# The per-layer gate and the router written as three products of high and low parts

## The chip, the cores and the metric

The kernel runs on one core of a Trainium2 chip. The metric is the device time of one execution in microseconds (us), the median of several runs. The engines are TensorE (PE: matmuls; its weight loads stand apart as PEld), VectorE (DVE), ScalarE (ACT), GpSimd (POOL) and SyncE (SP), which here only issues transfers from main memory.

## The reference, cut to what matters

The program is a two-layer block (feed-forward, mixers, attention) followed by one block with a mixture of experts, on 256 positions (two halves of 128, called t = 0 and 1) with 1024 features, all in 32-bit floats. The change lies in the last part of the second block:

```python
h = layer_norm_2(DEEPNORM_ALPHA_2 * h + y, ln1_g[i], ln1_b[i])
e = jnp.matmul(p[i], ple_proj[i]) * jax.nn.sigmoid(jnp.matmul(h, ple_gate[i]))
m = moe_ffn(h, w_router, router_bias, exp_w_up[i], exp_w_down[i])
h = layer_norm_2(DEEPNORM_ALPHA_2 * h + m + e, ln2_g[i], ln2_b[i])
...
aff = jax.nn.sigmoid(jnp.matmul(xt, w_router).astype(jnp.float32))      # in moe_ffn
```

`ple_gate` (1024 x 1024) is the gate of the per-layer input; `w_router` (1024 x 16) chooses two of 16 experts for each position. An expert has an up matrix of 1024 x 1024 and a down matrix of 512 x 1024.

## The kernel before, in words

**Two kinds of product.** Most products before the mixture are written as three products of parts: each operand is split into a high part, rounded to the type fp32r by ACT (`split`, L593), and a low part, the rest, by DVE (L594), and PE adds high x high, high x low and low x high (`mm3`, L598 to L600). For weights of the stream (`ws`) the casts are L298 and the subtractions L306. In the last part, the gate, the router and the experts are plain 32-bit float products.

**The weights of the last part** come in tiles of 128 x 2048 floats (1 MB), 102 of them, numbered in the order of their use: 0 and 1 are the left half of the gate, 2 the left half of the projection (`wp`, half as large), 3 to 8 expert 0 (four of up, two of down), 9 to 14 expert 1, 15 and 16 the right half of the gate, 17 the right half of the projection, 18 to 23 expert 2, and so on up to 96 to 101 of expert 15. `wtile` gives a tile its place in memory. The first `MOE_TILES` = 17 tiles have places of their own: 4 early ones (`w0` to `w3`), 4 slots of the stream's ring (a slot is a pair of half tiles, `wh` and `wl`), 3 buffers `raw` of the stream, and 6 more ring slots. A ring slot comes free when its last piece of the stream has been used, a `raw` buffer when its pieces have been split. From tile 17 on a tile takes the place of one that was given back with `moe_free`, in that order; SP issues all these loads in the order of the program (L245), and each waits until its place is free.

**The order of the work around the change** (`second`, L1790 and on) is that of the program on every engine. PE runs the out projection `w2`: for half 0, then for half 1. While it runs for half 1, DVE normalises half 0 (`ln_math`, L675 to L685, gain and bias in `gb`, loaded by SP). PE then turns the normalised X0 (`xT_plain`, into `xh`), runs `router(0)` (L1787) and five eighths of the gate's left half for t = 0 (`gate`, L1937). DVE meanwhile normalises X1. PE turns X1, ends the gate for t = 0, runs `router(1)` and the gate for t = 1. In `routing` DVE ranks the experts in some thirty short steps (from L1981 to L2009), PE counts positions (L2012 to L2016), DVE builds the selection S (L2091), and PE gathers the positions of the first four experts (`gather_quad`, L2104).

**The loop over 16 experts** (`moe`) follows: up products (L2135), then the down products (L2158) of the expert before, and the combining. After expert 0 stands the left projection, ahead of expert 2 (`GATE_AT`) the gate's right half for both t and the right projection.

Of the kernel before, what the change touches and what calls it, by code (L numbers as in the profile page):

```python
# [17 lines left out]
KT = 8  # L18
# [143 lines left out]
ALPHA2 = 2.0 ** 0.25  # L162
MOE_TILES = 17
MOE_EARLY = 4
# [345 lines left out]
class Kernel:  # L510
# [1245 lines left out]
    def w2(self, ks, ts, mid=None):  # L1756
        for k in ks:
            h, w = self.st.get(("w2", k))
            for t in ts:
                s = slice(t * P, (t + 1) * P)  # L1760
                for i in range(2):
                    c = slice(i * 512, (i + 1) * 512)
                    self.mm3(self.wacc[t][i], self.mix[0][:, k, s], self.mix[1][:, k, s], h[:, c], w[:, c],
                             k == 0, k == 7)
            if ts[-1]:
                self.st.release(("w2", k))
                self.moe_adv()
            self.st.pump(1)
            if mid and k == mid[0]:
                mid[1]()  # L1770

    def xT_plain(self, t, ss=(0, 1)):
        nc = self.nc
        for s in ss:
# [4 lines left out]
            pv = pt.rearrange("p (k n) -> p k n", k=4)  # L1779
            nc.scalar.copy(self.xf[:, 4 * s:4 * s + 2, t * P:(t + 1) * P], pv[:, 0:2])  # L1780
            nc.vector.tensor_copy(self.xf[:, 4 * s + 2:4 * s + 4, t * P:(t + 1) * P], pv[:, 2:4])

    def router(self, t):
        if t == 0:
            self.rps = self.mm()
        for k in range(KT):
            self.nc.tensor.matmul(self.rps[:, 16 * t:16 * t + 16], self.xf[:, k, t * P:(t + 1) * P],  # L1787
                                  self.rw[:, 16 * k:16 * k + 16], start=k == 0, stop=k == KT - 1)

    def second(self, g, acc, fs, fe):  # L1790
# [37 lines left out]
        self.ln_math(0, self.wacc[0], s2, e2)  # L1828
        self.xf = self.common.tile([P, KT, T], F32, name="xh")
        self.w2(range(2, 8), (1,), (6, lambda: self.xT_plain(0, (0,))))  # L1830
        self.xT_plain(0, (1,))
        self.p_T()
        self.m2ctx.close()
        self.moe_load(MOE_TILES)
        self.pe = self.pool("expert", 1, self.moectx, side="right")
# [21 lines left out]
    def moe_open(self):  # L1857
# [18 lines left out]
        self.wkind = [("early", f"w{i}", 0) for i in range(MOE_EARLY)]  # L1876
        self.wkind += [("ring", i % RING, i) for i in range(at - RING + RING_LESS, at)]
        self.wkind += [("raw", "raw", 0)] * RAWB
        self.wkind += [("ring", self.st.slot(i)[0], i) for i in range(n - RING_LESS, n)]
        assert len(self.wkind) == MOE_TILES  # L1880
        self.moe_load(MOE_EARLY)

    def wtile(self):
        i = len(self.wslot)
        s = i if i < MOE_TILES else self.wslot[self.wfree[i - MOE_TILES]]
        self.wslot.append(s)
# [26 lines left out]
    def moe_adv(self):  # L1913
        st = self.st
        while len(self.wtiles) < MOE_TILES:
# [3 lines left out]
            self.moe_load(len(self.wtiles) + 1)  # L1919

    def moe_free(self, tiles):
        self.wfree += tiles
        self.moe_load(MOE_TILES + len(self.wfree))

# [8 lines left out]
    def gate(self, i, t, ks):  # L1933
        for k in ks:
            w = self.wtiles[GATE_TILES[2 * i + k // 4]]
            c = k % 4 * 512
            self.nc.tensor.matmul(self.gacc[t], self.xf[:, k, t * P:(t + 1) * P], w[:, c:c + 512],  # L1937
                                  start=k == 0, stop=k == 7)

# [243 lines left out]
    def moe(self):  # L2183
        nc = self.nc
        self.nmm = 3
        self.gate_out()
        self.moe_free(GATE_TILES[:2])
        xg = self.gather_quad(0)
# [5 lines left out]
        for e in range(16):  # L2194
            if e == GATE_AT:
# [6 lines left out]
                next(ple)  # L2202
                self.moe_free(GATE_TILES[2:] + PROJ_TILES[1:])
            ps = self.mm()
# [36 lines left out]
            if e % 2 == 0:  # L2241
                self.prep(e // 2)
            if e in (7, 8):
                next(spill)
# [227 lines left out]
```

## Time and profile before

| what | value |
|---|---|
| time, median of 3 runs (lowest, highest) | 1537.07 us (1536.45 to 1538.68) |
| profiled execution, its own time | 1537.33 us |
| span of its profile, first to last instruction | 1535.5 us |
| PE busy | 1503.7 us, 98% of the span |
| DVE, ACT busy | 885.0 us, 654.2 us |
| read from main memory | 330.34 MB |

The span is what the trace shows; the 1.8 us between it and the execution's own time lie outside the program. All stretches are counted in us from the first instruction. The stretch of the change begins with half 1 of `w2` at about 1243 us and ends with the last expert at about 1522 us. PE's ends are modelled, so that a PE without idle time is best read from the starts of its instructions.

### The profile page before, as it was taken

How to read it: one execution, taken by the hardware profiler on the slowest of the kernel's cores; microseconds unless marked ns; L12 is line 12 of the kernel's file. 1: busy time of each engine (PE TensorE's matmuls, PEld its weight loads, DVE VectorE, ACT ScalarE, POOL GpSimd, SP SyncE). 2: the span in 40 equal slices, each digit the busy share in tenths (PEclk: the TensorE clock that was granted, in tenths of full speed). 3: DMA queues.
4: the chain of work that ended last, by engine and by line, in shares of the span. 5: the costliest groups of instructions: out<-in, count | busy, mean ns of one | idle time of the engine just before them, and what ended most of it. 6: DMA issues, size and time to landing. Idle time of an engine off the chain costs nothing. (4 is left out here: it accounts for less than half of the span.)

```text
span 1535.5 us, 23692 instructions
## 1 busy us (share of the span) xinstructions
PE 1503.7 (98%) x9717; PEld 1241.3 (81%) x9718; DVE 885.0 (58%) x1410; ACT 654.2 (43%) x1060; POOL 39.4 (3%) x61
## 2 busy tenths in 40 slices
PE   9999999999999999999999999999999999999996
PEld 7999989889999899998878999967989974434432
DVE  5644567785455745458857555568888465222223
ACT  5544435454443534336653434465774431111111
POOL 0000000000000000001001000020000000000000
PEclk9999999999999999999999999999999999999999
DMA  8654535555545554536334654545544677899991
GB/s 305 231 222 180 192 111 219 192 195 191 190 175 182 211 197 172 206 138 230 125 127 188 219 186 172 192 135 179 211 147 177 232 274 294 338 416 418 416 416 72
DMA packets 56130, 332.98 MB, mean 217 GB/s; under 512 B 6337, under 2 KB 6657, under 8 KB 24657
## 3 DMA queue, kind: packets, MB, share of 16 engines
q1 hardware_dynamic: 53568, 319.68, 55.4%
q0 software_dynamic: 1872, 9.52, 1.7%
q10 hardware_dynamic: 576, 2.22, 0.4%
q8 instruction: 78, 1.28, 0.3%
q14 instruction: 36, 0.29, 0.1%
HBM read 330.34 MB, written 1.05 MB: 216 GB/s over the span
## 5 line engine op out<-in xcount | busy, mean ns | idle before, releaser
L306 DVE TENSOR_TENSOR wl<-raw,wh 128x1024 fp32r<-128x1024 f32 (+1 forms) x403 | 474.1, 1216 | 130.4 <-ACT wh L298 130.0
L298 ACT CAST wh<-raw 128x1024 fp32r<-128x1024 f32 (+1 forms) x404 | 403.6, 1044 | 136.8 <-PE acc L600 45.6
L608 PE MATMUL mm<-xh,wh 128*128 128x256 f32 x1608 | 454.4, 283 | 2.0 <-DVE big L962 1.1
L609 PE MATMUL mm<-xl,wh 128*128 128x256 f32 x1608 | 451.7, 281 | 0.0
L610 PE MATMUL mm<-xh,wl 128*128 128x256 f32 x1608 | 451.2, 281 | 0.0
L608 PEld LDWEIGHTS mm<-xh,wh 128*128 128x128 f32 x1608 | 303.4, 189 | 7.5 <-issue 1.8
L609 PEld LDWEIGHTS mm<-xl,wh 128*128 128x128 f32 x1608 | 303.0, 188 | 2.0
L610 PEld LDWEIGHTS mm<-xh,wl 128*128 128x128 f32 x1608 | 303.5, 189 | 0.0
L422 ACT ACTIVATE fs<-mm 128x256 f32<-128x256 f32 x80 | 30.8, 385 | 280.6 <-PE mm L610 280.6
L424 DVE TENSOR_TENSOR fm<-fs,mm 128x256 f32<-128x256 f32 x80 | 33.6, 421 | 198.7 <-ACT fs L422 198.7
L599 PE MATMUL acc<-wl,fhh 128*128 128x512 f32 x352 | 139.1, 395 | 0.0
L598 PE MATMUL acc<-wh,fhh 128*128 128x512 f32 x352 | 138.9, 395 | 0.0
L600 PE MATMUL acc<-wh,fhl 128*128 128x512 f32 x352 | 138.5, 394 | 0.0
L600 PEld LDWEIGHTS acc<-wh,fhl 128*128 128x128 f32 x352 | 66.1, 188 | 15.6
L598 PEld LDWEIGHTS acc<-wh,fhh 128*128 128x128 f32 x352 | 66.3, 188 | 13.2
L599 PEld LDWEIGHTS acc<-wl,fhh 128*128 128x128 f32 x352 | 66.1, 188 | 12.8
L594 DVE TENSOR_TENSOR fhl<-fm,fhh 128x256 fp32r<-128x256 f32 x80 | 34.0, 426 | 37.7 <-ACT fhh L593 37.7
L2139 ACT ACTIVATE es<-mm 128x256 f32<-128x256 f32 x16 | 6.1, 384 | 109.1 <-PE mm L2135 109.1
L593 ACT CAST fhh<-fm 128x256 fp32r<-128x256 f32 x80 | 32.5, 406 | 45.1 <-DVE fm L424 45.1
L2173 DVE SCALAR_TENSOR_TENSOR X<-mm,ws,X 64x512 fp32r<-64x512 f32 x32 | 24.0, 750 | 42.5 <-ACT X L2170 41.9
L661 POOL TENSOR_TENSOR rs_r<-rs_v,nhalf 128x1 f32<-128x1 f32 (+3 forms) x21 | 17.8, 848 | 1167.0 <-DVE rs_v L659 1127.8
L2170 ACT ACTIVATE X<-mm,ws 64x512 fp32r<-64x512 f32 x32 | 21.9, 683 | 53.9 <-PE mm L2158 53.6
(603 smaller groups left out, 2112.5 us busy)
## 6 DMA issues: line engine op xcount, KB each, us to landing
raw<-in_ws_dram SPq DMA_DIRECT2D x196, 1024.0 KB, 4.9
wh<-in_we_dram SPq DMA_DIRECT2D x57, 512.0 KB, 11.3
wl<-in_we_dram SPq DMA_DIRECT2D x57, 512.0 KB, 11.2
w<-in_we_dram SPq DMA_DIRECT2D x22, 1024.0 KB, 11.9
raw<-in_we_dram SPq DMA_DIRECT2D x17, 1024.0 KB, 11.3
gb<-in_lnp_dram POOLq DMA_DIRECT2D x5, 1024.0 KB, 5.0
w<-in_wg_dram SPq DMA_DIRECT2D x2, 1024.0 KB, 7.5
raw<-in_ws_dram SPq DMA_DIRECT2D x2, 896.0 KB, 4.6
```

The source lines that it names most:

```text
L298: self.nc.scalar.copy(h[:, :n], src)
L306: self.eng.tensor_sub(l, src, h)
L422: nc.scalar.activation(s[:, :n], ps[:, :n], AF.Silu)
L424: nc.vector.tensor_tensor(m[:, :n], s[:, :n], ps[:, n:2 * n], op=OP.mult)
L593: self.nc.scalar.copy(h, src)
L594: self.nc.vector.tensor_sub(l, src, h)
L598: mm(out, lh, rh, start=first, stop=False)
L599: mm(out, lh, rl, start=False, stop=False)
L600: mm(out, ll, rh, start=False, stop=last)
L608: mm(out, h[:, c], xh[:, k, s], start=k == 0, stop=False)
L609: mm(out, h[:, c], xl[:, k, s], start=False, stop=False)
L610: mm(out, l[:, c], xh[:, k, s], start=False, stop=k == kn - 1)
```

## The change

The gate's and the router's products become `mm3`, three fp32r products each. For that:

- X0 and X1, when turned, are split into `xf` (high, ACT) and `xl2` (low, DVE); `xl2` takes the third `raw` buffer.
- The router's weights `rw` are split once, in `router(0)`.
- The gate's weight tiles are split in halves of 128 x 1024 by a generator, `presplit`, into four ring slots (`wh` and `wl` of each: the high and the low part). Tiles 0 and 1 are split in four steps during `w2` for half 1, tile 15 at the end of expert 0, tile 16 at the end of expert 1. A tile's place is given back as soon as it is split.
- These four ring slots and the third `raw` buffer are no longer among the first places, so that `MOE_TILES` is 12; they join (as -1 to -5 in `moe_free`) after the gate's right half.

```diff
-MOE_TILES = 17
+MOE_TILES = 12
...
             self.st.pump(1)
+            if not ts[0] == 0 and 1 < k < 6:
+                next(self.gsplit)
...
-            nc.scalar.copy(self.xf[:, 4 * s:4 * s + 2, t * P:(t + 1) * P], pv[:, 0:2])
-            nc.vector.tensor_copy(self.xf[:, 4 * s + 2:4 * s + 4, t * P:(t + 1) * P], pv[:, 2:4])
+            for k in (0, 2):
+                d = slice(None), slice(4 * s + k, 4 * s + k + 2), slice(t * P, (t + 1) * P)
+                self.split(self.xf[d], self.xl2[d], pv[:, k:k + 2])
...
+        if t == 0:
+            self.rhl = self.pe.tile([P, 2, P], F32R, name="eh", bufs=2)
+            self.split(self.rhl[:, 0], self.rhl[:, 1], self.rw)
         for k in range(KT):
-            self.nc.tensor.matmul(self.rps[:, 16 * t:16 * t + 16], self.xf[:, k, t * P:(t + 1) * P],
-                                  self.rw[:, 16 * k:16 * k + 16], start=k == 0, stop=k == KT - 1)
+            s, c = slice(t * P, (t + 1) * P), slice(16 * k, 16 * k + 16)
+            self.mm3(self.rps[:, 16 * t:16 * t + 16], self.xf[:, k, s], self.xl2[:, k, s], self.rhl[:, 0, c],
+                     self.rhl[:, 1, c], k == 0, k == KT - 1)
...
+    def presplit(self, i):
+        for t in GATE_TILES[2 * i:2 * i + 2]:
+            for h in range(2):
+                j = self.nstage % 4
+                hi, lo = [self.ringp.tile([P, 1024], F32R, name=s) for s in self.stages[2 * j:2 * j + 2]]
+                self.split(hi, lo, self.wtiles[t][:, h * 1024:(h + 1) * 1024])
+                self.wsplit[t, h] = hi, lo
+                self.nstage += 1
+                if h:
+                    self.moe_free([t])
+                yield
...
         for k in ks:
-            w = self.wtiles[GATE_TILES[2 * i + k // 4]]
-            c = k % 4 * 512
-            self.nc.tensor.matmul(self.gacc[t], self.xf[:, k, t * P:(t + 1) * P], w[:, c:c + 512],
-                                  start=k == 0, stop=k == 7)
+            h, l = self.wsplit[GATE_TILES[2 * i + k // 4], k % 4 // 2]
+            c, s = slice(k % 2 * 512, k % 2 * 512 + 512), slice(t * P, (t + 1) * P)
+            self.mm3(self.gacc[t], self.xf[:, k, s], self.xl2[:, k, s], h[:, c], l[:, c], k == 0, k == 7)
...
-        self.moe_free(GATE_TILES[:2])
+        next(self.gsplit, None)
+        self.gsplit = self.presplit(1)
...
-                self.moe_free(GATE_TILES[2:] + PROJ_TILES[1:])
+                self.moe_free([-1, -2, -3, -4, -5] + list(PROJ_TILES[1:]))
...
+            if e < GATE_AT:
+                next(self.gsplit)
+                next(self.gsplit)
```

DVE between the end of X0's normalisation (L685 on `X_72`) and the start of X1's (L675 on `X_73`), removed rows with -, new ones with +; `wl` from `w` is a low part of the gate's tiles 0 and 1, `raw` is `xl2`, `eh` the router's low part:

```order
 L685 SCALAR_TENSOR_TENSOR X_72<-X_72,rs_r,gb 128x512
-L1781 COPY xh<-acc 128x2x128 x2
-L1837 CAST identr<-ident 128x128
+L594 TENSOR_TENSOR wl_12616<-w_11646,wh_12615 128x1024
+L594 TENSOR_TENSOR wl_12630<-w_11646,wh_12629 128x1024
+L594 TENSOR_TENSOR wl_12644<-w_11648,wh_12643 128x1024
+L594 TENSOR_TENSOR wl_12658<-w_11648,wh_12657 128x1024
+L594 TENSOR_TENSOR raw<-acc,xh 128x2x128 x4
+L1848 CAST identr<-ident 128x128
+L594 TENSOR_TENSOR eh<-rw,eh 128x128
 L675 SCALAR_TENSOR_TENSOR X_73<-acc,X_73 128x512 x2
```

Nine subtractions now stand between the two normalisations, where two copies stood; the router's low part is the last of them.

SP around the load of `gb` for these normalisations; `in_ws` is the stream, `in_we` the experts' weights, and the removed ring rows shown are the last two of eight:

```order
-L245 DMA wh_12384<-in_we_dram 128x1024
-L245 DMA wl_12385<-in_we_dram 128x1024
-L285 DMA raw<-in_ws_dram 128x2048
-L245 DMA raw<-in_we_dram 128x2048 x3
+L285 DMA raw<-in_ws_dram 128x2048 x9
+L245 DMA raw<-in_we_dram 128x2048 x2
 L586 DMA gb<-in_lnp_dram 128x2048
```

Four ring tiles ahead of the last block of the stream are gone, and one load of 1 MB less stands ahead of `gb`.

SP from tile 13 to tile 20 in the changed kernel, with what each waits for (DMAHW: an earlier transfer; PE, DVE: the last use of the place):

```order
L245 DMA w_12710<-in_we_dram 128x2048 [waits DMAHW6_49,DVE_49]
L245 DMA w_13035<-in_we_dram 128x2048 [waits DMAHW7_49,PE_49]
L245 DMA raw<-in_wg_dram 128x2048 [waits DMAHW0_49,PE_49]
L245 DMA raw<-in_wg_dram 128x2048 [waits DMAHW1_49,PE_49]
L245 DMA wh_13041<-in_wp_dram 128x1024 [waits DMAHW2_49,PE_49]
L245 DMA w_13056<-in_we_dram 128x2048 [waits DMAHW3_49,PE_49]
L245 DMA raw<-in_we_dram 128x2048 [waits DMAHW4_49,DMAHW0_49,DVE_49]
L245 DMA wh_13113<-in_we_dram 128x1024 [waits DMAHW5_49,PE_49]
```

Tile 13 takes the place of tile 1 when that is split; tiles 14 to 17 take those of expert 0's up tiles, tile 18 that of the left projection, and tile 19 that of tile 15 when it is split, ahead of tile 20 and all that follow.

## Rows read from the trace of the kernel before

**Rows 1.** Page, section 1: busy time, share of the span, instructions.

```profile
PE 1503.7 (98%) x9717; PEld 1241.3 (81%) x9718; DVE 885.0 (58%) x1410; ACT 654.2 (43%) x1060; POOL 39.4 (3%) x61
```

**Rows 2.** PE's timeline: start, length, operation, count, idle time before and who ended it.

```profile
1244.63 0.39 PE L600 MATMUL acc<-wh,cz 128*128 128x512 f32 x1
...
1250.07 0.39 PE L600 MATMUL acc<-wh,cz 128*128 128x512 f32 x1
...
1253.43 1.86 PE L1787 MATMUL mm<-rw,xh 128*128 128x16 f32 x16
1255.13 4.54 PE L1937 MATMUL acc<-w,xh 128*128 128x512 f32 x10
...
1260.34 0.66 PE L1777 MATMUL acc<-ident,X 128*128 128x128 f32 x4 [0.23 <-DVE X L685]
...
1263.41 1.85 PE L1787 MATMUL mm<-rw,xh 128*128 128x16 f32 x16
...
1270.95 0.40 PE L2012 MATMUL mm<-r_o,tri 128*128 128x16 f32 x2 [0.44 <-DVE r_o L2009]
...
1273.49 0.80 PE L2104 MATMUL mm<-S,xl 128*128 128x256 f32 x2
```

**Rows 3.** DVE's timeline, same columns.

```profile
1236.88 4.63 DVE L306 TENSOR_TENSOR wl<-raw,wh 128x1024 fp32r<-128x1024 f32 x4 [2.02 <-ACT wh L298]
...
1249.01 0.75 DVE L684 SCALAR_TENSOR_TENSOR X<-X,ln_mv,gb 128x512 f32<-128x512 f32 x1 [3.00 <-DMA gb<-in_lnp_dram]
...
1251.33 0.75 DVE L685 SCALAR_TENSOR_TENSOR X<-X,rs_r,gb 128x512 f32<-128x512 f32 x1
1252.00 0.42 DVE L1781 COPY xh<-acc 128x256 f32<-128x256 f32 x1
...
1254.07 1.28 DVE L675 SCALAR_TENSOR_TENSOR X<-acc,X 128x512 f32<-128x512 f32 x2
...
1259.54 0.75 DVE L685 SCALAR_TENSOR_TENSOR X<-X,rs_r,gb 128x512 f32<-128x512 f32 x1
...
1272.72 0.76 DVE L2091 TENSOR_TENSOR S<-misc,r_rk 128x256 fp32r<-128x256 f32 x2
```

**Rows 4.** ACT's timeline, same columns.

```profile
1251.38 0.37 ACT L1780 COPY xh<-acc 128x256 f32<-128x256 f32 x1 [11.69 <-PE acc L1777]
```

**Rows 5.** SP's timeline: the issue of gb's load.

```profile
1242.03 0.33 SPq L586 DMA_DIRECT2D gb<-in_lnp_dram  x1
```

**Rows 6.** PE's timeline: the gate's right half, first and last stretch.

```profile
1301.27 1.98 PE L1937 MATMUL mm<-wh,xh 128*128 128x512 f32 x4
...
1315.11 3.60 PE L1952 MATMUL mm<-w,pT 128*128 128x512 f32 x8
```

**Rows 7.** Stretches: length, busy time by engine, PE's clock, share of transfers, GB/s.

```profile
1280.00:1325.00 45.00, 45.00 (x162) 17.59 (x160) 20.03 (x59) 5.81 (x10) 0.00 (x0) 1.00 0.88 331
1325.00:1485.00 160.00, 160.00 (x824) 66.90 (x819) 38.17 (x80) 25.17 (x44) 1.57 (x4) 1.00 1.02 417
```

**Rows 8.** SP's timeline: tiles 18 and 19, then 93.

```profile
1274.09 5.99 SPq L245 DMA_DIRECT2D w<-in_we_dram  x2
...
1468.18 0.33 SPq L245 DMA_DIRECT2D w<-in_we_dram  x1
```

**Rows 9.** Transfers issued within 1468.1 to 1468.6 us (tile 93): size, us to landing.

```profile
w<-in_we_dram SPq DMA_DIRECT2D x1, 1024.0 KB, 12.3
```

**Rows 10.** PE's timeline: the first use of tile 93, in expert 14.

```profile
1487.21 1.89 PE L2135 MATMUL mm<-w,xg 128*64 128x512 f32 x8
```

**Rows 11.** Stretch of the only fall of PE's clock inside the program.

```profile
1028.00:1032.00 4.00, 2.40 (x9) 1.82 (x9) 1.22 (x1) 4.00 (x10) 0.00 (x0) 0.71 0.92 248
1032.00:1036.00 4.00, 4.00 (x17) 3.22 (x15) 1.36 (x2) 3.30 (x10) 0.00 (x0) 0.86 0.56 230
```

**Rows 12.** PE's timeline there.

```profile
1027.15 1.36 PE L1304 MATMUL acc<-ident,X 128*128 128x128 f32 x8 [0.72 <-ACT X L1295]
1030.11 1.22 PE L627 MATMUL mm<-wh,xh 128*128 128x512 f32 x2 [1.60 <-ACT xh L1308]
```

More of the change, by code (lines that the diff above doesn't have):

```diff
@@ L1828, in second @@
         self.ln_math(0, self.wacc[0], s2, e2)
-        self.xf = self.common.tile([P, KT, T], F32, name="xh")
+        self.xf = self.common.tile([P, KT, T], F32R, name="xh")
+        assert len(self.wtiles) >= MOE_EARLY + RAWB - 1
+        self.xlt = self.rawp.tile([P, BLOCK], F32R, name="raw")
+        self.xl2 = self.xlt.rearrange("p (k n) -> p k n", k=KT)
+        self.gsplit = self.presplit(0)
         self.w2(range(2, 8), (1,), (6, lambda: self.xT_plain(0, (0,))))
@@ L1833, in second @@
         self.m2ctx.close()
-        self.moe_load(MOE_TILES)
+        self.moe_load(MOE_TILES + len(self.wfree))
         self.pe = self.pool("expert", 1, self.moectx, side="right")
@@ L1876, in moe_open @@
         self.wkind = [("early", f"w{i}", 0) for i in range(MOE_EARLY)]
-        self.wkind += [("ring", i % RING, i) for i in range(at - RING + RING_LESS, at)]
-        self.wkind += [("raw", "raw", 0)] * RAWB
+        self.wkind += [("raw", "raw", 0)] * (RAWB - 1)
+        later = range(at - RING + RING_LESS, at)
+        self.stages = [f"w{x}{i % RING}" for i in later for x in "hl"]
+        self.nstage, self.wsplit = 0, {}
         self.wkind += [("ring", self.st.slot(i)[0], i) for i in range(n - RING_LESS, n)]
         assert len(self.wkind) == MOE_TILES
+        self.wkind += [("ring", i % RING, i) for i in later] + [("raw", "raw", 0)]
         self.moe_load(MOE_EARLY)
@@ L1884, in wtile @@
         i = len(self.wslot)
-        s = i if i < MOE_TILES else self.wslot[self.wfree[i - MOE_TILES]]
+        s = i
+        if i >= MOE_TILES:
+            f = self.wfree[i - MOE_TILES]
+            s = self.wslot[f] if f >= 0 else MOE_TILES - 1 - f
         self.wslot.append(s)
@@ L1919, in moe_adv @@
             self.moe_load(len(self.wtiles) + 1)
+    def presplit(self, i):
[9 more added lines that the diff above has]
+                yield
     def moe_free(self, tiles):
         self.wfree += tiles
-        self.moe_load(MOE_TILES + len(self.wfree))
+        if len(self.wtiles) >= MOE_TILES:
+            self.moe_load(MOE_TILES + len(self.wfree))
     def p_T(self):
```

## Prediction

> **What bounds the kernel now.** I read the page's first section, then PE's timeline over the stretch of the change, then DVE's and SP's beside it, and last the loads of the expert weights against their use. PE is busy for 98% of the span [rows 1]: to shorten PE's work shortens the program, unless what PE waits for becomes late. The second timeline shows how close that is. Around the routing, PE's own work and DVE's chain are almost equally long: PE waits 0.23 us for X1 at 1260.34, 0.44 us for the ranking at 1270.95 [rows 2], and the gather starts at 1273.49, as DVE ends S (1272.72 + 0.76 = 1273.48) [rows 3]. In the expert loop the transfers run at 331 GB/s up to 1325 us and at 417 GB/s after that [rows 7], all that the core gets, so they are full; but PE has no idle time there, so they are not late. How far ahead they are: tile 93, issued at 1468.18 [rows 8], lands 12.3 us later [rows 9], at 1480.5, and is used at 1487.21 [rows 10]: 6.7 us. The leads shrink towards the end, and this is the smallest that I found. So three clocks run side by side: PE, DVE's chain into the routing, and the loads.
>
> **What the gate's products give.** In `w2` 24 fp32r products of 512 columns lie between the starts 1244.63 and 1250.07 [rows 2]: 5.44 / 24 = 0.227 us. The gate's right half takes 1315.11 - 1301.27 = 13.84 us for 16 plain products [rows 6], 0.865 us each. As 48 products at 0.227 it takes 10.88: 2.96 us less. The left half saves as much, 5.9 us in all.
>
> **The router.** Eight plain products of 16 columns take 1255.13 - 1253.43 = 1.70 us [rows 2], two passes each, 0.106 us a pass. Now there are 24 per half. With 16 columns the columns cannot be what sets the pace, so I take 0.106 each: 2.55 us, 0.85 more, twice. The ends: as much shorter as a gate product (0.227 / 0.865), 24 x 0.056 = 1.3 us; or the pace of 512 columns, 24 x 0.227 = 5.4 us. The Trainium skill, "TensorE: Matmul & The Clock Gate", section "Weight-path perf modes — Fast Weight Load (FWL) and DoubleRow", has weights of 128 columns that are not plain FP32 loaded faster, about twice as fast as measured there. By that the router would take about 1.3 us, my lower end, and the sum would come out 1.3 to 2.5 us lower; no row here has an fp32r product with so few columns.
>
> **DVE's chain into X1.** X0 comes earlier: DVE stands 3.00 us for `gb` at 1249.01 [rows 3], which SP issued at 1242.03 [rows 5] behind the third `raw` load. That load is gone, and with it 1 MB ahead of `gb`, 2.5 us at 417 GB/s [rows 7]: X0 ends at 1249.6 instead of 1252.1 (1251.33 + 0.75 [rows 3]). But ahead of X1 stand now four subtractions of 1024 columns (four took 4.63 us [rows 3]), four lows of X0 (0.36 us apart by the 0.42 us copy [rows 3], 1.5 together) and two short steps (0.3): X1 starts at 1256.0 instead of 1254.07 [rows 3]. X1 is then ready at 1262.2 instead of 1260.3: 1.9 us later. The four casts of tiles 0 and 1 cost ACT nothing: it stood idle for 11.69 us ahead of 1251.38 [rows 4], and some 4 us of casts fit there.
>
> **PE up to the gather.** PE is done with turning X0 and `p` at about 1253.0, as before, and then stands: its first router product needs the cast router weights (ACT, about 1254.3), its second the low part, DVE's last step before X1, at 1256.0. So PE idles about 1.3 and 1.7 us with one product between. Then router(0) to 1258.5, 15 gate products (3.4) to 1261.9, X1 turned at 1262.3 to 1262.8, 9 gate products (2.0) to 1264.8, router(1) to 1267.4. Before, router(1) ended at 1263.41 + 1.70 = 1265.1 [rows 2]. The ranking, the counts and S follow that end, so the gather starts 2.3 us later, at 1275.8. The gate's own gain there is all waited away: PE stands about 1.6 us for the ranking.
>
> **The clock.** It fell once inside the program, from 2.4 to 1.2 GHz, after PE had stood 0.72 and 1.60 us with 1.36 us of work between [rows 12]; two stretches show 0.71 and 0.86 of it granted [rows 11], so 4 x 0.29 + 4 x 0.14 = 1.7 us were lost. The new wait ahead of the router is longer, and the router's products fill little of the array. I take one such fall: about 1.6 us more, since it also covers the 0.4 us that PE would wait for X1. The gather starts 3.9 us later. With the right half's 2.96 PE enters expert 2 0.9 us later than before.
>
> **The weights.** When expert 0 gives its first place back, tile 19 is issued before (second of the pair from 1274.09 [rows 8]) and tile 14 now: tiles 14 to 18, one of half the size, are 4.5 x 2.51 = 11.3 us of transfer more to come. Tile 19 waits for the split of tile 15, and all behind it on SP too; DVE ends that split at about 1293.2 plus the shift, and I reckon 2.2 us of idle transfers for it. Against that, transfers are idle before for 45 x (1 - 331 / 417) = 9.3 us between 1280 and 1325 [rows 7], and will not be now: the loads run on to the end. 11.3 + 2.2 - 9.3 = 4.2 us later than the shift of expert 0; with 3.9, 8.1. The lead is 6.7 and PE itself is 0.9 late: PE waits 8.1 - 7.6 = 0.5 us in experts 14 and 15. If a quarter of the 9.3 cannot be used, it waits 2.8; if the split of tile 15 blocks nothing, none. The splits of tiles 15 and 16 themselves, 2.3 us of DVE each at the pace of rows 3, lie beside PE's work: between 1280 and 1325 DVE is busy for 20.03 of 45 us and ACT for 5.81 [rows 7]. I cost them at nothing beyond tile 19; without that cover expert 0's down product would wait up to 2.3 us.
>
> **The sum**, against the profiled execution's own 1537.33 us: + 2.3 (chain to the gather, with both routers and the left half in it) + 1.6 (clock) - 2.96 (right half) + 0.5 (weights) = + 1.4, so 1538.7. The median of the runs is 0.26 lower than that execution: **1538.5 us**, no change that can be measured (a measurement tells about 0.2%, 3.1 us, from none).
>
> **The rivals.** (1) Slower: PE's clock stays low for twice as long, because the router itself, at half speed, leaves the array idle, and falls again where PE stands for the ranking. Each costs another 1.7 us: + 1.4 + 3.4 = + 4.8, 1541.9. It decides from a second lost 1.7 us on. For it: the waits are longer than the one that sufficed [rows 12]. Against: before, PE stood 0.44 us and ran tiny products at 1270.95 [rows 2] at full clock. Chance 0.20. (2) Slower: the weights. The lead of 7.6 us is used up, and each further us is PE's wait; with tile 15's split 3 us late (ACT or DVE behind the projection's output), + 4.3, 1541.4. Chance 0.10. (3) Still the same: the clock holds and the router takes 1.3 us, the lower end: 1.4 - 1.6 - 1.3 (router(1); router(0) then waits for DVE) = - 1.5, 1535.6. Chance 0.08. (4) Faster: DVE's extra work hides altogether, so that both halves' 5.9 us stay, less 1.7 for the routers: - 4.2, and about 0.7 of waiting for weights: 1533.6. Against it stands DVE's order: nine subtractions ahead of X1, at a pace that rows 3 show. Chance 0.08. (5) The change doesn't do what it says: fp32r gate products run no faster in threes than one plain one. Rows 2 and 6 speak against it. Chance 0.02, some 1544.
>
> **How the numbers follow.** The forecast has 0.52. Same: 0.52 + 0.08 = 0.60. Slower: 0.20 + 0.10 + 0.02 = 0.32. Faster: 0.08. The range goes from 1534.0, which leaves out most of (4), to 1543.0, which takes in (1) and (2) with a longer wait for weights.
>
> **What would show it.** Right: `gb` lands near 1246.5; X1's first step on DVE near 1256; PE idle about 3 us ahead of router(0), ended by DVE's `eh`; a stretch of low clock after it; the right half of the gate in 10.9 us; the transfers at 417 GB/s from about 1297 on; PE's first waits for expert weights in experts 13 to 15. Wrong: a gather before 1274, PE waits for weights already before expert 10, or a left half that costs PE more than 3.4 + 2.0 + 5.4 us.

## The result and the profile after

The changed kernel takes **1545.84 us** (median of 5 runs, 1545.07 to 1546.17), the kernel before 1537.07: a ratio of 1.0056 [1.0045, 1.0067], 8.8 us slower. The forecast was 1538.5, with a range up to 1543.0. The profiled execution has a span of 1544.0 us, 8.5 more than before; its lines are compared with those of before. Line numbers are those of the changed kernel (gate and router L598 to L600 by `mm3`, the experts' up products L2164, the turning of X L1779, the gather L2133).

PE is still busy for 98% of the span, 1506.8 us (before, 1503.7). One execution of e4 below was in a slow state (8293.69 us) and is left out of its numbers.

PE's timeline from the turning of `p` to the gather (start, length, operation, count, idle time before and who ended it; beside rows 2):

```profile
1253.04 0.60 PE L1959 MATMUL mm<-ident,pin 128*128 128x128 f32 x4
1257.35 0.28 PE L598 MATMUL mm<-eh,xh 128*128 128x16 f32 x1 [3.72 <-ACT eh L593]
...
1257.81 0.26 PE L600 MATMUL mm<-eh,raw 128*128 128x16 f32 x1
...
1258.48 0.26 PE L600 MATMUL mm<-eh,raw 128*128 128x16 f32 x1
...
1261.72 0.77 PE L598 MATMUL acc<-wh,xh 128*128 128x512 f32 x1
...
1269.98 0.17 PE L598 MATMUL mm<-eh,xh 128*128 128x16 f32 x1
...
1272.82 0.77 PE L598 MATMUL acc<-wh,xh 128*128 128x512 f32 x1
...
1278.51 0.40 PE L2041 MATMUL mm<-r_o,tri 128*128 128x16 f32 x2
...
1281.13 0.41 PE L2133 MATMUL mm<-S,xl 128*128 128x256 f32 x2
```

`p` is turned as early as before, but the gather starts at 1281.13 instead of 1273.49 [rows 2]: 7.64 us later. PE stands for 3.72 us ahead of router(0); then the router's products start 0.67 / 6 = 0.112 us apart up to 1258.48, and twice as far apart behind that. The stretches of low clock (length, busy time of PE, PEld, DVE, ACT and POOL, PE's granted clock, share of transfers, GB/s):

```profile
1258.80:1265.40 6.60, 6.60 (x24) 5.83 (x24) 4.40 (x9) 0.00 (x0) 1.40 (x2) 0.50 1.04 419
1265.60:1272.20 6.60, 6.60 (x45) 5.85 (x43) 3.27 (x6) 2.34 (x5) 0.00 (x0) 1.00 0.40 169
1272.40:1275.60 3.20, 3.20 (x10) 2.62 (x11) 2.50 (x17) 0.69 (x2) 0.00 (x0) 0.50 0.00 0
1268.00:1287.00 19.00, 19.00 (x110) 15.58 (x110) 11.96 (x49) 5.73 (x11) 0.00 (x0) 0.91 0.02 7
```

PE runs at 1.2 GHz (0.50) for 6.8 us from 1258.7 on, and again for 3.4 us from 1272.3 on: 10.2 us, of which PE loses half, 5.1. The second time no wait stands ahead: 24 products of the router do. The last row shows the transfers: from 1268 to 1287 they carry 7 GB/s, since all places are full (before, 193 GB/s in the same stretch).

Where the 7.64 us come from is read at the first gate product behind router(1). Before, it started at 1265.12:

```profile
1265.12 5.40 PE L1937 MATMUL acc<-w,xh 128*128 128x512 f32 x12
```

Now it starts at 1272.82, 7.70 us later. The terms up to there: PE's wait, 3.72 instead of 0.23 for X1 [rows 2], + 3.5; two routers of 24 products at 0.111, 2.67 instead of 1.70 each, + 1.9; the gate's 24 products for t = 0 at 0.2335, 5.6 instead of 8 x 0.865 = 6.9, - 1.3; half of the 7.3 us of low clock up to there, + 3.65; together + 7.75.

Behind it the gather takes as long to come as before, 8.31 us instead of 8.37, though nearly all of the second fall lies there. DVE's ranking sets the pace: its last step starts at 1278.26 and takes 0.19 us, and PE takes up the counts (L2041) at 1278.51, right behind it. At full clock PE would have been there earlier and would have waited. So PE loses 5.1 us to the clock, but the gather only 3.65 (e6 shows the other case).

Behind the gather, the right half takes 1320.72 - 1309.51 = 11.21 us instead of 13.84 [rows 6], 2.63 less:

```profile
1309.51 0.50 PE L598 MATMUL mm<-wh,xh 128*128 128x512 f32 x1
...
1320.72 3.60 PE L1981 MATMUL mm<-wh,pT 128*128 128x512 f32 x8
```

Last, PE's waits from 1240 to 1530 us (who waits for whom: us in total, times, longest):

```profile
PE mm L598 <- ACT eh L593: 3.7, 1, 3.7
...
PE mm L2164 <- DMA raw<-in_we_dram: 1.0, 2, 0.6
PE mm L2164 <- DMA w<-in_we_dram: 0.9, 1, 0.9
PE mm L2176 <- DVE sg L1987: 0.8, 1, 0.8
```

PE waits for expert weights (L2164), as it did nowhere before, in experts 14 and 15: 1.8 us in three waits; between expert 14's start (5.6 us later than before) and the last down product (8.2 later) it loses 2.6. The 0.8 us for `sg` is the left projection's output, behind tile 15's split on DVE. Expert 0 starts 7.25 us later than before (the gather itself is 0.4 shorter), so + 7.25 - 2.6 + 0.8 + 2.6 = + 8.0 of the 8.5 of the spans; where the other 0.5 lie is not shown.

### The profile page after: what moved, and what is told of

Same layout as the page of the kernel before. It is cut to its first block, busy times and chain, and to the rows that moved or that the text cites. A ratio compares the mean times of both kernels' runs of the same rounds, so it can differ in the third digit from the quotient of the medians.

```text
span 1544.0 us, 23807 instructions
## 1 busy us (share of the span) xinstructions
PE 1506.8 (98%) x9765; PEld 1253.3 (81%) x9766; DVE 896.0 (58%) x1423; ACT 662.9 (43%) x1073; POOL 39.5 (3%) x61
## 3 DMA queue, kind: packets, MB, share of 16 engines
q8 instruction: 78, 1.28, 0.3%
## 5 line engine op out<-in xcount | busy, mean ns | idle before, releaser
L598 PE MATMUL acc<-wh,fhh 128*128 128x512 f32 x352 | 138.8, 394 | 0.0
L600 PE MATMUL acc<-wh,fhl 128*128 128x512 f32 x352 | 138.7, 394 | 0.0
L600 PEld LDWEIGHTS acc<-wh,fhl 128*128 128x128 f32 x352 | 66.1, 188 | 15.5
L598 PEld LDWEIGHTS acc<-wh,fhh 128*128 128x128 f32 x352 | 66.3, 188 | 13.1
L2169 DVE TENSOR_TENSOR es<-es,mm 128x256 f32<-128x256 f32 x16 | 6.7, 421 | 65.5 <-ACT es L2168 65.5
```

Of the source, the lines that this page charges most:

```text
L598: mm(out, lh, rh, start=first, stop=False)
L600: mm(out, ll, rh, start=False, stop=last)
```

## The experiments

Three causes were to be told apart: PE's wait, with DVE's longer way to X1; the clock, and whether PE's wait or the router's own small products let it fall; and the weights, with their five missing places. All times are beside runs of the kernel before on the same chip, which took 1536.55 to 1537.32. Executions of one of these kernels differ by 3 us and more, in part from work ahead of the change: DVE's first step of X0's normalisation (L675), which no edit here touches, starts between 1239.76 (e7) and 1245.37 us (e1) in the profiled executions, at 1243.02 in the kernel before and at 1243.48 in the changed one. So where times lie close the traces decide, and stretches up to the gather are counted from that step ("from X0's normalisation"): 30.5 us before, 37.65 in the changed kernel.

### e1: the places alone

```diff
 # before, and only this
-MOE_TILES = 17
+MOE_TILES = 12   # four ring slots and the third raw buffer join after the right half
```

> The kernel before, with nothing changed but the places of the expert weights: the third raw buffer and four ring slots join only after the gate's right half, as in the changed kernel; all products are as before. My theory: the changed kernel waits about 2.6 us for weights in experts 14 and 15 because PE itself enters expert 0 7.2 us late there and the loads, which start when expert 0 gives its first place back, are late by that and by about 7 us more; without the late start of PE the fewer places cost loads about 5 us of lateness, less than the 6.7 us by which tile 93 is ahead before, so PE waits for nothing: 1537 to 1537.7, within 0.2% of before. Rival: the fewer places alone cost the 2.6 us, so 1539.7, with waits for weights in experts 14 and 15.

Measured: 1537.12, ratio 1.0000 [0.9990, 1.0009]. PE's waits from 1281 to 1530 hold no transfer:

```profile
PE mm L2162 <- DVE eh L2153: 1.2, 1, 1.2
PE acc L2184 <- DVE X L2177: 0.2, 1, 0.2
```

Five places fewer cost nothing by themselves; the last weights land 7.6 us later than before (1510.6 instead of 1503.0), of which 2 us are this execution's own later start of expert 0, and the lead covers it. The waits of the changed kernel come from the late start of its loop on top of that.

### e2: a third of the router's products

```diff
-            self.mm3(self.rps[:, 16 * t:16 * t + 16], ...)
+            self.nc.tensor.matmul(self.rps[:, 16 * t:16 * t + 16], self.xf[:, k, s], self.rhl[:, 0, c], ...)
```

> The changed kernel with a third of the router's products: high x high alone, 8 per half instead of 24 (left out: the two products with low parts; which experts are chosen can differ a little). Theory A, the router's own 24 products of 16 columns let PE's clock fall: in the changed kernel the second fall (1272.3, 3.4 us long) comes with no wait ahead of it, so with 8 products, 0.9 us, it doesn't come, and router(0) ends before the clock can fall or falls once for shorter. Then 1.8 us less per router, 1.7 us for the second fall and perhaps 1.7 for the first: 1540 to 1542. Theory B, PE's wait of 3.7 us ahead of router(0) lets it fall: the first fall stays 6.8 us long, and only the shorter routers count, about 1542.5 to 1544.

Measured: 1543.08, 1.0036 [1.0025, 1.0048]. PE's two waits in its timeline, and three stretches with their granted clock (columns as above):

```profile
1257.12 1.06 PE L1794 MATMUL mm<-eh,xh 128*128 128x16 f32 x8 [3.75 <-ACT eh L593]
...
1274.14 0.40 PE L2041 MATMUL mm<-r_o,tri 128*128 128x16 f32 x2 [2.74 <-DVE r_o L2038]
```

```profile
1258.70:1262.00 3.30, 3.30 (x10) 2.52 (x9) 2.78 (x7) 0.00 (x0) 1.41 (x2) 0.50 1.02 407
1262.20:1275.60 13.40, 10.66 (x60) 8.76 (x59) 9.74 (x38) 3.01 (x7) 0.00 (x0) 1.00 0.44 183
1275.80:1279.00 3.20, 3.20 (x12) 2.71 (x12) 0.92 (x4) 0.60 (x1) 0.00 (x0) 0.50 0.00 0
```

Neither theory has it whole. With eight products no fall follows router(1), as A wanted; but the clock falls behind each of the two waits, as B wanted, the first time for 3.4 us and not for B's 6.8. The second wait is new: PE, faster now, stands for the ranking. So a wait can let the clock fall; whether the row alone can is e4's question.

### e3: the router's products among the gate's

```diff
-        self.router(0)
-        self.gate(0, 0, range(5))
+        self.router(0, mid)   # after each k: one or two of the 15 gate products
...
-        self.gate(0, 0, range(5, 8))
-        self.router(1)
+        self.router(1, mid)   # after each k: one or two of the 9 gate products
```

> The changed kernel with the same products in another order on PE alone: after each three products of router(0) stand one or two of the 15 gate products that followed it, and after each three of router(1) one or two of the 9 gate products that stood ahead of it; the wait of 3.7 us ahead of router(0) is left. Theory A (the 24 small products in a row let the clock fall): no second fall, the first one gone or half as long; 3.4 to 5.1 us of low clock less, of which PE waits about 1.5 back for the ranking: 1542 to 1543.5. Theory B (the wait lets it fall): the first fall stays at 6.8 us; a gain of at most 1.7: 1544 to 1546.

Measured: 1549.28 (4 runs, 1545.45 to 1551.80), 1.0085 [1.0068, 1.0102]: a miss, slower than the changed kernel. The wait ahead stayed (3.73 us). In the profiled execution, the fastest of the four, the low clock lasts 10.2 us in one piece:

```profile
1257.00:1267.00 10.00, 10.00 (x36) 8.63 (x36) 4.23 (x8) 0.00 (x0) 1.41 (x2) 0.50 0.94 383
```

A clock that was already low was not brought back sooner by wide products among the small ones. That the mix keeps it down for longer is not shown: e6 and e12, without it, had 10.2 us in one piece too. The two slowest executions had a mean granted clock of 0.987 and 0.989 over the span, the other two 0.992 and 0.993; where they lost it is not recorded.

### e4: the wait ahead of router(0) taken away

```diff
-            self.rhl = self.pe.tile(...); self.split(self.rhl[:, 0], self.rhl[:, 1], self.rw)   # in router(0)
+        self.rhl = self.rt.tile([P, 4, P], F32R, name="sg"); self.split(...)                    # while w2 runs
...
+            for k, d in zip((0, 2), ds): self.nc.scalar.copy(self.xf[d], pv[:, k:k + 2])        # both casts,
+            for k, d in zip((0, 2), ds): self.nc.vector.tensor_sub(self.xl2[d], ...)            # then both lows
...
-        self.split(hi, lo, ...)                     # all four gate subtractions ahead of X0's lows
+        self.subs_do(1); xT_plain(0, (0,)); self.subs_do(1); ...; xT_plain(0, (1,)); ...; self.subs_do(2)
```

> The changed kernel with DVE's and ACT's steps ahead of router(0) in another order: the router's weights are split while w2 runs, two of the four subtractions for the gate's tiles stand behind the lows of X0, and both casts of a turned block stand ahead of both its lows. All products stay. Both theories: PE's wait of 3.7 us ahead of router(0) is gone or under 0.6 us, router(0) starts at about 1253.6, X1's first step on DVE stays near 1257.3. Theory A (the small products let the clock fall): it falls in or right behind router(0) all the same, and again at router(1); 3 to 4 us less than the changed kernel, about 1542. Theory B (the wait lets it fall): no first fall, PE then stands about 3.5 us for X1; about 1541, and a fall after that wait.

Measured: 1542.5 (4 runs, 1541.30 to 1544.16), 1.0039 [1.0023, 1.0055]; the gather starts at 1276.63, 33.3 us from X0's normalisation, 4.3 less than in the changed kernel. The wait is gone and router(0) ends at 1255.9, behind 24 products without a gap; right there the clock falls, and again behind router(1) (stretches, columns as above):

```profile
1250.00:1255.80 5.80, 5.80 (x46) 5.32 (x44) 5.08 (x9) 2.78 (x7) 0.00 (x0) 1.00 0.98 373
1256.10:1259.30 3.20, 3.20 (x8) 2.53 (x9) 3.20 (x6) 0.00 (x0) 0.00 (x0) 0.50 1.03 413
1269.70:1272.90 3.20, 3.20 (x9) 2.45 (x9) 2.69 (x17) 0.00 (x0) 0.00 (x0) 0.50 0.00 0
```

A row of 24 small products can be enough without a wait (A); it isn't always, since the same row kept a full clock at router(0) in e9 and at router(1) in e6, e7 and e12. Without the wait there are 6.8 us of low clock, in two pieces, instead of 10.2. The second piece costs nothing here either: the gather comes 8.35 us behind router(1). The Trainium skill, "TensorE: Matmul & The Clock Gate", section "HAM oscillation — how this bites in real kernels", has PE's waits for data let the clock fall, so that the next work starts cold. The rows of e2 agree with that (0.50 behind 3.75 and 2.74 us of waiting); those of e4 show that it is not the only way.

### e5: e4 with a shorter row

```diff
+            for x in (self.xf, self.xl2):   # 16 products of 32 columns [high | low] per half
+                self.nc.tensor.matmul(o, x[:, k, s], self.rhl[:, 0:2, c], ...)
...
+        nc.vector.reduce_sum(sel, lg.rearrange("p t h e -> p t e h"), axis=AX.X)
```

> As e4, and the router as 16 products of 32 columns per half instead of 24 of 16: the high and the low part of a weight stand side by side, so that the high and the low part of x each meet both at once (low x low comes with it), and DVE adds the two sums in one more short step. Theory A (a row of small products that lasts over 2 us lets the clock fall): 16 of them last about 1.8 us, as the router of the kernel before, which ran at full clock; so no fall at either router, two times 1.7 us less of lost clock and 0.9 us less per router; PE then waits about 2 us more for X1, so 2 to 3 us less than e4, 1539 to 1541. Theory C (any row of small products behind a stretch of other work lets it fall): both falls stay, 1541 to 1542.5.

Measured: 1544.58, 1.0046 [1.0029, 1.0062]: no gain over e4, a miss for both. Router(0) with 16 products kept its clock. But PE, done earlier, now stands for X1 and for the ranking, and the clock falls behind each of these waits (at 1262.9 and at 1276.6, 3.4 us each):

```profile
1261.96 0.63 PE L1779 MATMUL acc<-ident,X 128*128 128x128 f32 x4 [2.99 <-DVE X L685]
...
1275.05 0.39 PE L2056 MATMUL mm<-r_o,tri 128*128 128x16 f32 x2 [1.62 <-DVE r_o L2053]
```

To shorten PE's work while DVE's chain sets the pace turned the gain into a wait, and the wait cost clock.

### e6: places given back early, the right half later

```diff
-GATE_AT = 2
+GATE_AT = 6
...
+        self.moe_free([-1, -2, -3, -4])                              # as soon as the left half is done
+        self.held = [_wtile(GATE_AT - 2, j) for j in range(4)]       # expert 4's places stage the right half
...
-                self.moe_free([-1, -2, -3, -4, -5] + list(PROJ_TILES[1:]))
+                self.moe_free(self.held + [-5] + list(PROJ_TILES[1:]))
```

> The changed kernel, with the places given back in another way: the four ring slots of the left half go to expert weights as soon as the left half is done, and the gate's right half (with its projection) stands ahead of expert 6 instead of expert 2, split in expert 5 into four places that expert 4 gave back. The part up to expert 0 is as in the changed kernel. My theory: PE's waits for weights in experts 14 and 15 (1.9 us, 2.6 with the small ones) come from the transfers that stand still between 1268 and 1287 us and again ahead of tile 19, since places are missing; here tiles 14 to 17 load from 1281 on, so these waits are gone: 1543 to 1543.5. If the wait of 0.77 us for the left projection (DVE was at tile 15's split) goes too, 1542.5. Rival: the loads are late by PE's own late start of the loop alone, and nothing is gained: 1545 to 1546.

Measured: 1541.78 (10 runs), 1.0032 [1.0021, 1.0044], 4.1 us less than the changed kernel with as much low clock in its profile (10.2 us). PE's waits over 0.3 us from 1240 to 1530 us, and its timeline from router(1) to the gather:

```profile
PE mm L598 <- ACT eh L593: 3.8, 1, 3.8
PE mm L2051 <- DVE r_o L2048: 1.3, 1, 1.3
PE mm L2197 <- DVE eh L2188: 1.2, 1, 1.2
```

```profile
1271.87 0.48 PE L598 MATMUL acc<-wh,xh 128*128 128x512 f32 x1
...
1277.57 0.40 PE L2051 MATMUL mm<-r_o,tri 128*128 128x16 f32 x2 [1.28 <-DVE r_o L2048]
...
1280.19 0.41 PE L2143 MATMUL mm<-S,xl 128*128 128x256 f32 x2
```

The waits for weights and for the left projection are gone; the last weights land at 1507.4 instead of 1517.7, and expert 0's start lies 255.3 us ahead of the span's end instead of 259.0. My theory of the weights holds, though the edit moves the right half along with the places. The gain is 0.7 us larger than the most I expected; X0's normalisation starts 1.4 us earlier in this execution, which would cover it.

The timeline also prices the changed kernel's second fall. Up to the gather the program is the same, but here the low clock lies in one piece from 1254.2 on, and none follows router(1). PE stands 1.28 us for the ranking instead, and the gather comes 8.32 us behind router(1), as with the fall (8.31).

### e7 and e8: GpSimd, and all together

```diff
 # e7: e4, and
-            self.nc.vector.tensor_sub(lo, src, hi)
+            (self.nc.gpsimd if t < 2 else self.nc.vector).tensor_sub(lo, src, hi)   # two ahead of X0's normalisation
...
+        self.xT_plain(1, (0,)); self.gate(0, 0, range(6, 7)); self.xT_plain(1, (1,))
 # e8: e7 with e5's router and e6's places
```

> As e4, and the four subtractions for the gate's tiles 0 and 1 on GpSimd, two of them ahead of X0's normalisation; X1 is turned in two parts between the gate's products. DVE then has only X0's lows and the short steps ahead of X1: X1's first step at 1254.5 instead of 1256.8, X1 ready at 1260. Both theories of the clock: the falls in router(0) and router(1) stay. The gather starts 1.5 to 2.5 us earlier than in e4: 1539 to 1541. Rival: GpSimd's subtractions slow DVE beside them, X1 comes no earlier: as e4, 1541.5 to 1543.5.

> e5, e6 and e7 together. If the three causes add up (PE's wait ahead of router(0) with DVE's longer way to X1; the clock that falls at the routers; the weights), PE reaches the gather as early as in the kernel before, about 1273.5 us, the right half gives its 2.6 us, and no wait for weights eats it: 1534 to 1535.5, faster than both kernels. If the clock still falls at the routers: 1537. If the weights still come late: about 1537 too, with waits in experts 14 and 15.

Measured: e7 1540.89, 1.0024 [1.0012, 1.0037]; e8 1539.80, 1.0009 [1.0000, 1.0019], e7 within its expected times, e8 4.3 us over. The timelines of DVE and GpSimd in e7 show one reason:

```profile
1244.19 2.70 DVE L685 SCALAR_TENSOR_TENSOR X<-X,rs_r,gb 128x512 f32<-128x512 f32 x1
1246.82 2.88 DVE L684 SCALAR_TENSOR_TENSOR X<-X,ln_mv,gb 128x512 f32<-128x512 f32 x1
```

```profile
1243.42 5.73 POOL L1961 TENSOR_TENSOR wl<-w,wh 128x1024 fp32r<-128x1024 f32 x2
```

While GpSimd subtracts, DVE's steps of the normalisation, which read X and `gb`, take 2.70 and 2.88 us instead of 0.75; X0 comes 4 us later than it could, and PE waits 1.5 us for it (1.35 in e8). The Trainium skill, "SBUF — State Buffer", section "SBUF: two separate sides", says that DVE and GpSimd share a pair of ports under an exclusive lock, which a DVE instruction with two inputs in SBUF takes against a GpSimd instruction that reads there; the two long steps fit that.

In e7 the clock fell only once up to the gather, for 3.4 us. The gather started at 1273.18, which looks as early as before (1273.49):

```profile
1239.76 1.37 DVE L675 SCALAR_TENSOR_TENSOR X<-acc,X 128x512 f32<-128x512 f32 x2 [1.51 <-PE acc L600]
```

```profile
1273.18 0.42 PE L2148 MATMUL mm<-S,xl 128*128 128x256 f32 x2
```

But this execution was 3.3 us ahead of the kernel before at X0's normalisation already. From there the gather takes 33.4 us, as in e4 (33.3), and X1's first step came 0.5 us earlier than in e4. So up to the gather GpSimd gave nothing that shows: the rival, that its work slows DVE's, is the mechanism, e7's time is in the range by luck, and its interval overlaps e4's. PE waits 1.9 us for weights in experts 14 and 15, as in the changed kernel. In e8 those waits are gone, but the clock was low for 6.8 us from the middle of router(0) on and for 3.4 behind a wait of 2.85 us for the ranking.

### e9 and e10: a version that beats both

```diff
 # e8, and in e9 the router's 24 products again
-            (self.nc.gpsimd if t < 2 else self.nc.vector).tensor_sub(lo, src, hi)
+            (self.nc.gpsimd if t == 0 else self.nc.vector).tensor_sub(lo, src, hi)   # GpSimd only ahead of X0's normalisation
...
+        self.nc.vector.tensor_sub(l[:, 0], self.X[0], h[:, 0])   # ahead of X1's lows
...
         self.gate(0, 1, range(6))
+        self.proj_t(0, 0)                                        # half of the left projection, ahead of the ranking's products
```

> A version meant to beat both kernels, with the router's 24 products of 16 columns. From e4, e6 and e7: the splits of X0 and of the router's weights early, tile 0's subtractions on GpSimd ahead of X0's normalisation only (in e7 and e8 the later two made DVE's L684 and L685 2.7 to 2.9 us long instead of 0.75, and PE waited 1.4 us for X0), tile 1's on DVE beside the casts; the right half ahead of expert 6; X0's low part for the gather ahead of X1's; and half of the left projection (4 products, 1.8 us) where PE waits for the ranking. Theory A: with no wait of PE ahead of it, the row of 24 small products still lets the clock fall once or twice (1.7 to 3.4 us): 1535 to 1537. Theory B (only waits let it fall): no fall at the routers, 1532.5 to 1534.

> As e9, with the router's 16 products of 32 columns. Theory A (the length of the row of small products counts): no fall at router(0) and router(1), the gather starts at about 1273, 2.6 us from the right half, 1.8 from the projection, no wait for weights: 1532.5 to 1534, 1.7 to 3.4 us less than e9 and faster than both kernels. Theory C (any such row lets it fall): as e9 less 1 us.

Measured: e9 **1534.10**, 0.9982 [0.9973, 0.9992]; e10 **1532.19**, 0.9967 [0.9956, 0.9979]: faster than both kernels, e10 by 4.4 us than the one before and by 13.7 than the changed one. In e10 PE has no wait over 0.3 us up to the gather, which starts at 1272.85, and none for weights behind it (PE's timeline, then PE's waits of 0.3 us and more from 1240 to 1530):

```profile
1272.85 0.41 PE L2171 MATMUL mm<-S,xl 128*128 128x256 f32 x2
```

```profile
PE mm L2225 <- DVE eh L2216: 1.2, 1, 1.2
PE mm L1793 <- DVE raw L1784: 0.3, 1, 0.3
```

Router(0) kept its clock in both. Behind router(1) it fell in both, for 3.4 us, so that e10's 16 products didn't save it, as A had it; e9's time lies between its two theories. Here the fall does cost about its 1.7 us, since half of the projection fills the wait for the ranking: the gather comes 10.05 and 10.02 us behind router(1). That the 1.9 us between the two times are the 2 x 8 x 0.111 = 1.8 us of fewer products is not shown: from X0's normalisation to the gather the two traces differ by 0.8 us, from expert 0 on by 0.1. Several edits are in here at once; the runs don't price each by itself.

### e11 and e12: mixed products on a full clock, and the changed kernel again

```diff
 # e11: e4 with e3's order of PE; e12: the changed kernel as it is
```

> e3 and e4 together: no wait of PE ahead of router(0), and the router's products among the gate's (one or two of 512 columns behind each three of 16). It tells whether e3's stretch of low clock, 10.2 us in one piece, came from its wait alone. If wide products among the small ones hold a clock that has not fallen: no fall from 1250 to 1266, PE then waits for X1 as in e4, 1540 to 1542. If they do not: a fall in router(0) as in e4 or longer, since the row of mixed products is longer: 1542 to 1545.

> The changed kernel once more, unchanged, beside e11 on the same chip. It tells how far its time and its stretches of low clock differ from one execution to the next: the time 1544.5 to 1547, PE's wait of 3.7 us ahead of router(0) the same, the low clock between 6.8 and 10.2 us in the stretch from 1256 to 1277.

Measured: e11 1545.72, 1.0054 [1.0036, 1.0073]; e12 1546.34 (1544.53 to 1550.09), 1.0053 [1.0033, 1.0073]. In e11 the mixed router(0) kept the full clock that it found, for 6.3 us up to PE's next wait; PE then waited 2.08 and 0.73 us for X1, the clock fell, and through the mixed router(1) it stayed low for 13.7 us, the longest stretch of all (columns as above):

```profile
1252.50:1261.60 9.10, 7.02 (x46) 5.84 (x44) 8.54 (x16) 2.02 (x5) 1.41 (x2) 1.00 1.03 415
1261.90:1275.20 13.30, 12.79 (x44) 11.31 (x45) 6.87 (x27) 2.84 (x7) 0.00 (x0) 0.50 0.42 176
```

So the mix did not let the clock fall by itself; in e3 it had fallen behind the wait. e11's time was a miss for me. e12's profiled execution, 1550.09, is the changed kernel with two long falls:

```profile
1256.60:1266.70 10.10, 8.65 (x32) 7.94 (x33) 6.67 (x14) 2.06 (x5) 1.41 (x2) 0.50 1.03 418
1280.50:1287.10 6.60, 6.60 (x26) 6.02 (x26) 1.22 (x5) 1.18 (x2) 0.00 (x0) 0.50 0.01 2
```

The same program, the same wait of 3.72 us, but 17.1 us of low clock instead of 10.2, with 4.25 us between the two executions. Of these, 0.7 lie ahead of the change (X0's normalisation starts at 1244.17 instead of 1243.48). The first fall is 3.4 us longer, but 1.5 us of it lie in PE's wait, and router(1) ends only 0.5 later. Behind router(1) the clock didn't fall this time; PE stood 1.27 us for the ranking, and then it fell for 6.8 us over the counts, the last gate products and the gather, where PE has no wait to take its place: PE loses half of it, 3.4, and expert 0 starts 3.1 later behind router(1) than in the changed kernel's profile. How often the clock falls, for how long and over which work differs between executions, and with it the price.

## Why the prediction was wrong, step by step

**The steps that failed are the clock, one fall counted and 1.6 us taken for it, and the chain into router(0).** From X0's normalisation the gather came after 37.65 us; the forecast, 1277.4, makes 34.4. Of the 3.3 us the clock has 2.0: 3.65 were lost up to router(1)'s end. The chain into router(0) has 1.2: its second product came 14.2 us behind X0's normalisation, forecast 13.0. The sizes of the products have 0.4, and the 0.4 us that PE was to wait for X1 didn't come.

That the clock could stay low for longer and fall a second time is rival (1), to which I gave 0.20. It had the first half right (6.8 us in one piece). The second fall came in router(1)'s last products and not at the wait for the ranking, and cost the gather next to nothing; that its price, 3.4 us more, is near the 3.5 by which PE's loss exceeds my 1.6 is luck. The step behind the chance was wrong: against a second fall I put that PE ran tiny products behind a wait of 0.44 us at full clock at 1270.95 [rows 2]. Those are a few products. In e4 the clock fell behind a row of 24 without a wait, in e2 behind waits with a short row. What decides stays open: the row of 24 kept the clock at router(0) in e9 and at router(1) in e6, e7 and e12, and 16 products kept it at router(0) in e5 and e10, not at router(1) in e10, nor at router(0) in e8, behind PE's wait of 1.35 us for X0.

**What I said PE would wait away** is lost as forecast, in another form. I let PE stand 1.6 us for the ranking; the second fall took the place of that wait. With it or without it the gather comes 8.3 us behind router(1) (8.31; e6 8.32; forecast 8.4), since DVE's ranking sets the pace there.

**DVE's chain into X1** was right in kind and too short: X1's first step came at 1257.54, forecast 1256.0, and 0.5 of the 1.5 us were there at X0's normalisation. `gb` came as forecast (issued at 1240.16), X0 ended at 1250.08 (forecast 1249.6), the four subtractions took 4.62 us. DVE's timeline behind them:

```profile
1250.00 4.62 DVE L594 TENSOR_TENSOR wl<-w,wh 128x1024 fp32r<-128x1024 f32 x4
1254.54 0.42 DVE L594 TENSOR_TENSOR raw<-acc,xh 128x256 fp32r<-128x256 f32 x1
1255.39 0.76 DVE L594 TENSOR_TENSOR raw<-acc,xh 128x256 fp32r<-128x256 f32 x2 [0.44 <-ACT xh L593]
1256.59 0.42 DVE L594 TENSOR_TENSOR raw<-acc,xh 128x256 fp32r<-128x256 f32 x1 [0.44 <-ACT xh L593]
...
1257.54 1.28 DVE L675 SCALAR_TENSOR_TENSOR X<-acc,X 128x512 f32<-128x512 f32 x2
```

The lows of X0 don't run back to back. They alternate with ACT's casts of the same block, each of which waits for the low before it; so the lows took 2.5 us, not 1.5, and the two short steps 0.6, not 0.3. e4, with both casts ahead of both lows and two subtractions beside the casts, had X1's first step at 1256.83, 13.5 us behind X0's normalisation instead of 14.1. For the same reason ACT ended the cast of the router's weights only at 1257.3, where I had 1254.3; PE's wait became 3.72 us in one piece instead of 1.3 and 1.7.

**The sizes of the products held.** A gate product took 0.2335 us (forecast 0.227): - 2.63 for the right half instead of - 2.96. A router product took 0.112 at full clock (forecast 0.106), 0.97 more per router instead of 0.85. The lower end, 0.056, which stood nearest to the Trainium skill's faster weight load ("TensorE: Matmul & The Clock Gate", section "Weight-path perf modes — Fast Weight Load (FWL) and DoubleRow"), was not seen: these fp32r products with few columns are no faster than a plain pass.

**The weights** were sized too small: 2.6 us instead of 0.5. Tile 93 landed 14.9 us after its issue at 1479.5, at 1494.4, just as PE took it up:

```profile
w<-in_we_dram SPq DMA_DIRECT2D x1, 1024.0 KB, 14.9
```

```profile
1494.42 1.94 PE L2164 MATMUL mm<-w,xg 128*64 128x512 f32 x8 [0.89 <-DMA w<-in_we_dram]
```

That is 13.9 us later than before, where I had 8.1; of the difference 3.4 us are expert 0's later start (7.25 instead of 3.9), which the loads follow. For the rest, the transfers carry 307 GB/s from 1285 to 1300 and 384 from 1301 to 1325 instead of 417: by my estimate some 6 us of standing still, where I had 2.2. My sign, 417 GB/s from about 1297 on, didn't come. Tile 19 waited for tile 15's split as forecast (issued at 1300.56, as DVE ended it). PE takes tile 93 up 7.2 us later than before, which is the 13.9 less the lead of 6.7: 5.6 are its own lateness at expert 14, 1.6 it lost there. e1 and e6 show both halves of it: fewer places alone cost nothing, a late loop with transfers kept going costs nothing.

**Tile 15's split** I costed at nothing beyond tile 19. Its two subtractions (2.36 us from 1298.17 on) stand ahead of the left projection's output on DVE, and PE waited 0.77 us for that, not at the down product where I had looked.

Together: 0.5 that were there ahead of the change, + 3.3 up to the gather, - 0.4 in the gather, + 0.3 right half, + 0.8 projection, + 2.1 weights: 6.6 of the 7.3 us by which the forecast missed.

## What to carry to other kernels

Ahead of a row of many small products, or a new wait of some microseconds, price PE's clock at each such place and not once: half of the low stretch is lost where it hits PE's work on the path, and nothing where PE would have waited behind it. Products that become cheaper on PE pay only as far as the other engines' chain and the loads get shorter too; here the same gate products, with the splits taken off DVE's chain, places given back early and a part of the projection moved into a wait, turned from 8.8 us slower into 4.4 us faster. Two engines that take turns on one block (cast, low, cast, low) cost a handover each; all casts first, then all lows, cost one.

## What was not expected of the hardware

- The clock fell behind 24 products of 16 columns with no wait ahead (e4 at 1256.0; the changed kernel at 1272.3), but not behind the same row at router(0) in e9 and at router(1) in e12. With small products spread among wide ones a full clock stayed full for 6.3 us, and a low one low for 13.7 (e11).
- Between two executions of the same program the low clock lasted 10.2 and 17.1 us (the changed kernel and e12), with 4.25 us between their times, of which 0.7 lie ahead of the change.
- GpSimd's subtractions of 128 x 1024 made DVE's steps of 128 x 512 with two inputs in SBUF 2.70 and 2.88 us long instead of 0.75 (e7).
